# A decoder layer's opening loads put in order of use on one queue, and its constants made during the down projection

## The chip, the cores and the metric

One core of one Trainium2 chip runs the whole kernel. The metric is the device time of one execution in microseconds (us). Matrix products run on TensorE (PE; PEld is its loading of the stationary operand), element-wise work on VectorE (DVE) and ScalarE (ACT). DMAs are issued from the instruction queues of SyncE (SP), ACT and GpSimd (POOL); an issue stands in that engine's order and waits there.

## The reference

One layer of a decoder, 256 tokens of width 2048, all in float32:

```python
h = LN1(ALPHA * x + 0.5 * swiglu(x, ffn1))            # FFN width 5632
mix = mixer(h)      # latent attention beside differential attention, gated and projected
h = LN2(ALPHA * h + mix)
h = LN3(ALPHA * h + 0.5 * swiglu(h, ffn2))

swiglu(x) = (silu(x @ w_gate) * (x @ w_up)) @ w_down
LN(z)     = (z - mean) * rsqrt(var + 1e-5) * g + b
rms(c)    = c * rsqrt(mean(c * c) + 1e-6) * g          # on the latent vectors, on the outputs of the second branch
```

The mixer needs constants that depend on the positions alone: a causal mask, a position bias for each of four heads, the sine and cosine of the rotary angles, and a scalar `lam` from four short vectors.

## The kernel before

**Products.** Each float32 operand is split into a high and a low part (`split`, L148: ACT copies to the PE's rounded type, DVE subtracts), and a product is three matmuls (`triple`, L201). Tokens are two blocks of 128. A weight unit is two k-tiles of 128 by 512 columns, 512 KB; for each unit and block there are six matmuls.

**Units and order.** `project` (L206) walks the units of one 512-column chunk. A unit has four steps: `load` (a DMA on SP into one of four `raw` buffers), `prep` (the split into a pair of a ring of `wring` tiles), the products of block 0, and, as a later step, those of block 1. `lag[0]` says by how many units block 1 may stay behind block 0 (`catch_up`, L163). Each unit ends in a `tick`, and `later(n, f)` puts work n ticks ahead. The program is written in this order; the compiler's scheduler gives each engine its own order from it and issues an instruction sooner if its inputs and a buffer for its output are free. Buffers are taken from pools by tag: `tmp` has six, `sm` 24, `cols` four.

**The opening.** PE first runs 16 matmuls on zeros (`WARM`, L34 and L97). x comes transposed as eight quarters of 256 KB, quarter q of block b by `load_x(q, b)` (L925), issued on ACT's queue: `load_x(0, 0)` before the first unit, the others from `start_hook` at units 1 to 6. The weights come on SP. The first FFN has 22 chunks of gate and up columns; the first two go through `project`, the rest in pairs through `Hybrid.group` (L282), in which part of the work takes seven products in place of eight with sums of weight blocks on DVE (L316).

**Constants.** `setup` (L604) is put 24 ticks ahead at the start (L936), which is in the gate and up stage. It loads the positions, the rotary frequencies, the four short vectors and the gain of the second branch by small DMAs on POOL's queue, and makes the constants on POOL, DVE and ACT.

**Down projection and norms.** `ffn` then sets the ring to four pairs (L571), makes a `LayerNorm` and walks four chunks of 22 units. The LayerNorm loads the residual rows `z` and the gain and shift as rows (`gb`, broadcast to 128 partitions) and, for LN1 and LN2, as columns (`cols`, two DMAs into the `cols` buffers); its `evac` adds each chunk to `z`, and `apply` normalizes, transposes on PE and scales by `cols`. `twice_rstd` (L380) takes one Newton step after a square root and returns twice the reciprocal root, so gains are halved beforehand on ACT (L438, L452, L709) or in `setup` (L658).

**Latent vectors.** In `mixer`, `ckv2_done` (L732) makes the rotary part of the keys, `kr_row`, and puts its transposes on PE (`to_cols`, L672) two ticks ahead.

Of the kernel before, what the change touches and what calls it, by code (L numbers as in the profile page):

```python
# [11 lines left out]
F32 = mybir.dt.float32  # L12
# [6 lines left out]
P = 128  # L19
# [11 lines left out]
G = 2  # L31
SLOTS = 40
LAG = 5
WARM = 16  # L34
# [25 lines left out]
def layer_kernel(ctx: ExitStack, tc: tile.TileContext, a: dict, out: bass.AP):  # L60
# [145 lines left out]
    def project(w, x, k_tiles, width, done, k0=0, hook=None):  # L206
# [15 lines left out]
        def one(j):  # L222
            st = {}

            def load():
                st["raw"] = wpool.tile([P, G * width], F32, tag="raw", name=nm("raw"), bufs=4)
                nc.sync.dma_start(st["raw"], w[j])
# [152 lines left out]
    def twice_rstd(v, eps, n, between=None):  # L380
# [48 lines left out]
    class LayerNorm:  # L429
        def __init__(self, scale, residual, g, bt, each, x=None, cols=None, at=(0, 8)):  # L430
# [41 lines left out]
        def apply(self, b):  # L472
# [5 lines left out]
            if self.cols is None:  # L478
# [3 lines left out]
                r = twice_rstd(mv[:, 1:2], LN_EPS, 1, lambda: center(0))  # L482
# [7 lines left out]
            r = twice_rstd(mv[:, 1:2], LN_EPS, 1)  # L490
# [12 lines left out]
    def ffn(n, x, wgu, wdn, residual, g, bt, each, first=None, nxt=None, cols=None):  # L503
# [52 lines left out]
        project(wgu[0], x, KD, 512, lambda b, bank: gu_done(0, b, bank), hook=first_hook)  # L556
# [47 lines left out]
    def setup():  # L604
# [4 lines left out]
        pos_i = sm(2, "pos_i", I32)  # L609
# [47 lines left out]
        nc.gpsimd.dma_start(subg, a["subln_g"].partition_broadcast(P))  # L657
        V.tensor_scalar(out=subg, in0=subg, scalar1=0.5 * (1.0 - LAMBDA_INIT), scalar2=None, op0=ALU.mult)  # L658
# [45 lines left out]
    def mixer(x):  # L704
# [4 lines left out]
        S.mul(gain, gain, 0.5)  # L709
# [3 lines left out]
        def c_norm(b, i):  # L713
# [6 lines left out]
            r = twice_rstd(ms, RMS_EPS, 1)  # L720
# [11 lines left out]
        def ckv2_done(b, bank):  # L732
# [7 lines left out]
            later(2, lambda: to_cols(kr, krT, b, 2))  # L740
# [70 lines left out]
        def diff_head(h):  # L811
# [24 lines left out]
            def values():  # L836
# [13 lines left out]
                r = twice_rstd(ms, RMS_EPS, 2)  # L850
# [74 lines left out]
    def load_x(q, b):  # L925
        raw = xq.raw(q, b) if q in xq.kept else tmp_tile([P, 512], "xraw")
        nc.scalar.dma_start(raw, a["xT"][q, b])
# [118 lines left out]
```

## Time and profile before

| What | us |
|---|---|
| three runs | 2028.65, 2031.71, 2031.77 |
| median | 2031.71 |
| the profiled execution, its own time | 2028.37 |
| its span, first to last instruction | 2026.6 |
| landing of a 512 KB gate/up weight unit, median of 192 | 4.4 |
| landing of a 256 KB quarter of x, median of 8 | 9.4 |
| idle time of DVE before the splits of weights, waiting for ACT | 409.8 |
| idle time of ACT before the casts of weights, waiting for PE | 540.5 |

The mean TensorE clock granted over the span is 0.997. The last two rows say that over the kernel as a whole ACT and DVE wait for PE to give back ring buffers, not the other way round; where that is not so, the stretches in the prediction show it. A stage is read from its own stretch: the share of busy time over the whole span mixes stages with different limits.

### The profile page before, as it was taken

To read this page: it belongs to the slowest core of one execution; us is meant where nothing else is said; L and a number is where in the kernel's file an instruction comes from. 1 tells how busy PE (TensorE), PEld (TensorE's weight loads), DVE (VectorE), ACT (ScalarE), POOL (GpSimd) and SP (SyncE) were. 2 spreads that over 40 slices of the span, in tenths; PEclk is the share of its full clock that TensorE was granted. 3 is DMA by queue.
4 is the path that set the end of the run, shared out by engine and by line. 5 is a ranking of instruction groups with operands and counts; after the bars stand their busy time and mean duration, and the time that the engine had idled before them with its cause. 6 is when DMAs were issued, how large, how long until landed. Compare 5 with 4: busy or idle time off the path is not lost.

```text
span 2026.6 us, 25079 instructions
## 1 busy us (share of the span) xinstructions
PE 2004.1 (99%) x8984; PEld 1659.3 (82%) x8984; DVE 1527.0 (75%) x1791; ACT 1151.3 (57%) x1443; POOL 218.6 (11%) x409
## 2 busy tenths in 40 slices
PE   8999999999999999999999999999999999999997
PEld 7788888888888887888888888878888888888886
DVE  6999999997554686655665555699999999964555
ACT  5666666676333565555674445476666666653332
POOL 0111001112000012520001100001100100220000
PEclk9999999999999999999999999999999999999999
DMA  8766766668666757874456685666776566686664
GB/s 285 235 223 223 242 227 200 214 218 304 204 195 191 244 183 247 289 246 150 158 167 218 206 282 187 214 232 219 248 248 220 195 216 236 207 309 192 193 196 136
DMA packets 129085, 445.79 MB, mean 220 GB/s; under 512 B 18544, under 2 KB 18624, under 8 KB 128960
## 3 DMA queue, kind: packets, MB, share of 16 engines
q1 hardware_dynamic: 108000, 387.50, 57.3%
q0 software_dynamic: 19808, 54.60, 8.6%
q10 hardware_dynamic: 1152, 2.10, 0.3%
q8 instruction: 70, 1.15, 0.2%
q14 instruction: 55, 0.45, 0.1%
HBM read 419.48 MB, written 24.64 MB: 219 GB/s over the span
## 4 chain that ended last, share of the span: by engine, by line
PE 92%; DMA 3%; DVE 3%; issue 1%; ACT 0%; POOL 0%; DVEq 0%; SPq 0%; ACTq 0%; POOLq 0%
PE mm L202 30%; PE mm L203 30%; PE mm L204 30%; DVE wring L150 1%; DMA xraw<-in_xT_dram 1%; DMA turn<-blocks 1%; DMA sraw<-in_gu_dram 1%; DVE sraw L316 1%; PE tr L370 0%; DMA z<-in_x_dram 0%; ACT wring L149 0%; PE tr L791 0%; PE tr L820 0%; PE tr L789 0%; DVE blocks L405 0%
## 5 line engine op out<-in xcount | busy, mean ns | idle before, releaser
L150 DVE TENSOR_TENSOR wring<-raw,wring 128x1024 fp32r<-128x1024 f32 (+1 forms) x582 | 701.6, 1209 | 409.7 <-ACT wring L149 404.8
L149 ACT CAST wring<-raw 128x1024 fp32r<-128x1024 f32 (+1 forms) x582 | 604.9, 1043 | 547.3 <-PE mm L204 470.1
L202 PE MATMUL mm<-wring,h 128*128 128x512 f32 (+2 forms) x1632 | 634.1, 389 | 0.0
L204 PE MATMUL mm<-wring,h 128*128 128x512 f32 (+2 forms) x1632 | 630.0, 386 | 0.0
L203 PE MATMUL mm<-wring,h 128*128 128x512 f32 (+2 forms) x1632 | 629.4, 386 | 0.7 <-DVE wring L150 0.7
L203 PEld LDWEIGHTS mm<-wring,h 128*128 128x128 f32 x1632 | 306.7, 188 | 62.3 <-DVE wring L150 1.9
L204 PEld LDWEIGHTS mm<-wring,h 128*128 128x128 f32 x1632 | 306.6, 188 | 62.1 <-DVE h L150 1.0
L202 PEld LDWEIGHTS mm<-wring,h 128*128 128x128 f32 x1632 | 306.7, 188 | 61.1 <-ACT h L149 1.0
L149 ACT CAST wring<-sraw 128x1024 fp32r<-128x1024 f32 x280 | 290.1, 1052 | 113.7 <-PE mm L204 70.4
L150 DVE TENSOR_TENSOR wring<-sraw,wring 128x1024 fp32r<-128x1024 f32 x280 | 335.2, 1219 | 7.3 <-ACT wring L149 4.9
L202 PE MATMUL mm<-wring,xs 128*128 128x512 f32 x560 | 218.0, 389 | 1.5 <-ACT snap L293 1.5
L203 PE MATMUL mm<-wring,xs 128*128 128x512 f32 x560 | 218.0, 389 | 0.8 <-DVE wring L150 0.8
L204 PE MATMUL mm<-wring,xs 128*128 128x512 f32 x560 | 217.9, 389 | 0.0
L316 DVE TENSOR_TENSOR sraw<-sraw,sraw 128x1024 f32<-128x1024 f32 x160 | 191.9, 1215 | 0.1
L407 POOL DMA_DIRECT2D hT<-blocks x176 | 95.5, 550 | 744.0 <-DVE blocks L405 739.9
L202 PE MATMUL mm<-wring,x 128*128 128x512 f32 x384 | 150.5, 393 | 4.4 <-ACT x L149 4.4
L203 PE MATMUL mm<-wring,x 128*128 128x512 f32 x384 | 150.1, 392 | 0.3 <-DVE wring L150 0.3
L204 PE MATMUL mm<-wring,x 128*128 128x512 f32 x384 | 150.0, 392 | 0.0
L202 PEld LDWEIGHTS mm<-wring,xs 128*128 128x128 f32 x560 | 105.1, 188 | 23.8 <-ACT snap L293 1.9
L203 PEld LDWEIGHTS mm<-wring,xs 128*128 128x128 f32 x560 | 105.1, 188 | 23.2 <-DVE wring L150 1.3
L204 PEld LDWEIGHTS mm<-wring,xs 128*128 128x128 f32 x560 | 105.1, 188 | 21.6
L407 POOL DMA_DIRECT2D turn<-blocks x104 | 56.6, 551 | 309.9 <-DVE blocks L405 271.1
(238 smaller groups left out, 1619.1 us busy)
## 6 DMA issues: line engine op xcount, KB each, us to landing
raw<-in_gu_dram SPq DMA_DIRECT2D x192, 512.0 KB, 4.4
raw<-in_dn_dram SPq DMA_DIRECT2D x176, 512.0 KB, 4.3
sraw<-in_gu_dram SPq DMA_DIRECT2D x160, 512.0 KB, 5.1
raw<-in_wgm_dram SPq DMA_DIRECT2D x32, 512.0 KB, 3.4
raw<-in_wgd_dram SPq DMA_DIRECT2D x32, 512.0 KB, 3.9
raw<-in_w_out_dram SPq DMA_DIRECT2D x32, 512.0 KB, 3.4
hT<-blocks POOLq DMA_DIRECT2D x176, 64.0 KB, 2.5
hraw<-hT POOLq DMA_DIRECT2D x44, 256.0 KB, 4.1
```

The source lines that it names most:

```text
L149: S.copy(hi, src)
L150: V.tensor_tensor(out=lo, in0=src, in1=hi.bitcast(F32), op=ALU.subtract)
L202: PE.matmul(o, xh, wh, start=first, stop=False, skip_group_check=again)
L203: PE.matmul(o, xh, wl, start=False, stop=False, skip_group_check=again)
L204: PE.matmul(o, xl, wh, start=False, stop=last, skip_group_check=again)
L316: V.tensor_tensor(out=t, in0=t, in1=R[add[1]][s], op=ALU.add)
L407: nc.gpsimd.dma_start(to.rearrange("(g r) (i f) -> i r g f", g=4, i=4)[i], t[32 * i:32 * (i + 1), :].rearrange("r (g f) -> r g f", g=4))
```

## The change

- `WARM` goes from 16 to 12.
- All eight quarters of x are issued on SP's queue, between the weight units in the order of their use: `first_tokens` loads the quarter of block 0 ahead of an even unit, `second_tokens` (through the new argument `between`) that of block 1 just before block 1's products. The first unit is loaded and split in two halves. `lag[0]` is no longer set to 1 at the start, so in the first chunk block 1 follows block 0 unit by unit.
- `setup` is put 26 ticks ahead from the start of the first FFN's down projection. Its `pos_i` and the raw gain of the second branch are now `tmp` tiles.
- `twice_rstd` becomes `rstd`: the square root is taken of four times the value, so that the plain reciprocal root comes out, and the halvings of `cols`, `gb`, `gain` and `subg` go. `cols` is one DMA into a `tmp` tile.
- The transposes of `kr_row` are put four ticks ahead in place of two.

```diff
-WARM = 16
+WARM = 12
...
-    def project(w, x, k_tiles, width, done, k0=0, hook=None):
+    def project(w, x, k_tiles, width, done, k0=0, hook=None, between=None):
...
+            parts = [slice(i * width, (i + 1) * width) for i in range(G)] if between is not None and j == 0 else [slice(0, G * width)]
...
-                nc.sync.dma_start(st["raw"], w[j])
+                for c in parts:
+                    nc.sync.dma_start(st["raw"][:, c], w[j][:, c])
...
-                split(*pair, st["raw"])
+                for c in parts:
+                    split(*(t[:, c] for t in pair), st["raw"][:, c])
...
-            return load, prep, lambda: products(0, j, st["pair"]), lambda: products(1, j, st["pair"])
+            def second():
+                if between is not None:
+                    between(j)
+                products(1, j, st["pair"])
+            return load, prep, lambda: products(0, j, st["pair"]), second
...
-    def twice_rstd(v, eps, n, between=None):
+    def rstd(v, eps, n, between=None):
...
-        S.activation(sd, ve, AF.Sqrt)
+        S.activation(sd, ve, AF.Sqrt, scale=4.0)
...
-        V.tensor_scalar(out=w, in0=v, scalar1=eps, scalar2=-1.0, op0=ALU.add, op1=ALU.mult)
+        V.tensor_scalar(out=w, in0=v, scalar1=eps, scalar2=-4.0, op0=ALU.add, op1=ALU.mult)
...
-                self.cols = [small.tile([P, KD], F32, tag="cols", name=nm("cols"), bufs=4) for _ in range(2)]
-                for t, src in zip(self.cols, cols):
-                    nc.gpsimd.dma_start(t, src)
-                S.mul(self.cols[0], self.cols[0], 0.5)
+                t = tmp_tile([P, 2, KD], "cols")
+                nc.gpsimd.dma_start(t.rearrange("p a k -> p (a k)"), cols)
+                self.cols = [t[:, i, :] for i in range(2)]
...
-                if i == 0:
-                    later(4, lambda: S.mul(t, t, 0.5))
...
-        project(wgu[0], x, KD, 512, lambda b, bank: gu_done(0, b, bank), hook=first_hook)
+        project(wgu[0], x, KD, 512, lambda b, bank: gu_done(0, b, bank), hook=first_hook,
+                between=between)
...
+        if n == 1:
+            later(26, setup)
         for c in range(4):
             project(wdn[c], h, KF, 512, lambda b, bank, c=c: ln.evac(c, b, bank), hook=more if c == 0 else dn_hook(c))
...
-        pos_i = sm(2, "pos_i", I32)
+        pos_i = tmp_tile([P, 2], "pos_i", I32)
...
-        nc.gpsimd.dma_start(subg, a["subln_g"].partition_broadcast(P))
-        V.tensor_scalar(out=subg, in0=subg, scalar1=0.5 * (1.0 - LAMBDA_INIT), scalar2=None, op0=ALU.mult)
+        sg = tmp_tile([P, DV], "sg")
+        nc.gpsimd.dma_start(sg, a["subln_g"].partition_broadcast(P))
+        V.tensor_scalar(out=subg, in0=sg, scalar1=1.0 - LAMBDA_INIT, scalar2=None, op0=ALU.mult)
...
-        S.mul(gain, gain, 0.5)
...
-            later(2, lambda: to_cols(kr, krT, b, 2))
+            later(4, lambda: to_cols(kr, krT, b, 2))
...
-        nc.scalar.dma_start(raw, a["xT"][q, b])
+        nc.sync.dma_start(raw, a["xT"][q, b])
...
-    def start_hook(j):
-        if j in (2, 4, 6):
-            load_x(j // 2, 0)
-        if 1 <= j < 5:
-            load_x(j - 1, 1)
-
-    later(24, setup)
+    def first_tokens(j):
+        if j % 2 == 0:
+            load_x(j // 2, 0)
+
+    def second_tokens(j):
+        if j % 2 == 0:
+            load_x(j // 2, 1)
+
     set_ring(LAG + 5)
-    lag[0] = 1
-    load_x(0, 0)
```

More of the change, by code (lines that the diff above doesn't have):

```diff
@@ L481, in center @@
                                            op0=ALU.subtract, op1=ALU.mult)
-                r = twice_rstd(mv[:, 1:2], LN_EPS, 1, lambda: center(0))
+                r = rstd(mv[:, 1:2], LN_EPS, 1, lambda: center(0))
                 for c in range(4):
@@ L489, in apply @@
                 return
-            r = twice_rstd(mv[:, 1:2], LN_EPS, 1)
+            r = rstd(mv[:, 1:2], LN_EPS, 1)
             for c in range(4):
@@ L501, in apply, with ffn @@
                 later(12 + c, lambda c=c: finish(c))
-    def ffn(n, x, wgu, wdn, residual, g, bt, each, first=None, nxt=None, cols=None):
+    def ffn(n, x, wgu, wdn, residual, g, bt, each, first=None, between=None, nxt=None, cols=None):
         hb = {}
@@ L719, in c_norm @@
             V.tensor_scalar(out=ms, in0=ss, scalar1=1.0 / RANK, scalar2=None, op0=ALU.mult)
-            r = twice_rstd(ms, RMS_EPS, 1)
+            r = rstd(ms, RMS_EPS, 1)
             V.scalar_tensor_tensor(out=c, in0=c, scalar=r, in1=gain[:, i * RANK:(i + 1) * RANK],
@@ L849, in values @@
                 V.tensor_scalar(out=ms, in0=ss, scalar1=1.0 / DV, scalar2=None, op0=ALU.mult)
-                r = twice_rstd(ms, RMS_EPS, 2)
+                r = rstd(ms, RMS_EPS, 2)
                 orow = tmp_tile([P, 512], "orow")
@@ L952, in layer_kernel @@
     h2 = Acts(KD, "h2", (0, 1))
[L953 removed]
+    ln = LayerNorm(1.0, res[0], a["ln2_g"], a["ln2_b"], keep(1), h2, a["ln2_cols"])
     for c in range(4):
```

10 lines of the change are left out of this document (4 added, 6 removed).

## The prediction

> **What bounds the kernel now.** I read the page's engine table and chain first.
>
> ```profile
> PE 2004.1 (99%) x8984; PEld 1659.3 (82%) x8984; DVE 1527.0 (75%) x1791; ACT 1151.3 (57%) x1443; POOL 218.6 (11%) x409
> ...
> PE 92%; DMA 3%; DVE 3%; issue 1%; ACT 0%; POOL 0%; DVEq 0%; SPq 0%; ACTq 0%; POOLq 0%
> ```
>
> TensorE is busy for 2004.1 of 2026.6 us, so everything that this change can win lies in some 22 us: where PE is idle, where its clock is low, and before its first real product. Busy time by stretches shows where (columns: stretch, its length, busy time of PE, PEld, DVE, ACT, POOL, then PE clock, DMA share, GB/s).
>
> ```profile
> core 0: us, PE busy (x) PEld busy (x) DVE busy (x) ACT busy (x) POOL busy (x), PEclk, DMA share, GB/s
> ...
> 7.07:12.76 5.69, 5.37 (x24) 3.86 (x22) 3.13 (x6) 2.62 (x3) 0.00 (x0) 1.00 1.01 313
> 12.76:17.12 4.36, 0.00 (x0) 0.00 (x0) 1.25 (x2) 0.67 (x3) 0.00 (x0) 0.92 1.05 397
> 17.12:23.28 6.16, 6.16 (x15) 4.86 (x16) 5.81 (x8) 6.16 (x11) 0.00 (x0) 0.50 0.40 138
> ...
> 60.00:115.00 55.00, 52.65 (x231) 42.95 (x231) 52.42 (x83) 36.66 (x46) 12.54 (x23) 1.00 0.67 216
> 115.00:470.00 355.00, 355.00 (x1568) 293.87 (x1567) 347.70 (x358) 235.01 (x276) 42.18 (x78) 1.00 0.68 225
> 470.00:510.00 40.00, 39.32 (x173) 31.90 (x172) 25.12 (x29) 23.88 (x27) 10.73 (x20) 1.00 0.90 321
> 510.00:700.00 190.00, 190.00 (x840) 157.39 (x839) 97.82 (x87) 77.83 (x74) 0.00 (x0) 1.00 0.64 205
> ```
>
> The reader is to see: a hole of 4.36 us at 12.76, then 6.16 us in which PE is "busy" at clock 0.50, then 2.35 us lost in 60 to 115, 0.68 lost at the head of the down projection (470 to 510), and nothing in between. What opens the hole is in the timeline (start, duration, instruction, idle time before and what ended it) and, below the dots, in the chain of waits.
>
> ```profile
> 1.06 6.28 PE L98 MATMUL tr<-zero 128*128 128x128 f32 x32 [1.06 <-DVE zero L96]
> 5.02 0.86 ACTq L927 DMA_DIRECT2D xraw<-in_xT_dram  x2
> 11.33 0.33 ACTq L927 DMA_DIRECT2D xraw<-in_xT_dram  x1
> 11.71 1.05 ACT L149 CAST wring<-raw 128x1024 fp32r<-128x1024 f32 x1 [2.91 <-DMA xraw<-in_xT_dram]
> 16.45 2.18 ACT L149 CAST x<-xraw 128x512 fp32r<-128x512 f32 x4 [3.69 <-DMA xraw<-in_xT_dram]
> 17.12 1.22 PE L202 MATMUL mm<-wring,x 128*128 128x512 f32 x2 [4.36 <-ACT x L149]
> ...
> 7.24 9.19 DMA xraw<-in_xT_dram
> ```
>
> A quarter of x issued at 7.24 lands at 16.43. ACT both issues x and casts, in order: its last issue comes as late as 11.33, and the cast behind it stands 2.91 us on x. Weights of later units share the DMA engines meanwhile (SP issues them from 0.74 on, shown below). So PE starves for x, not for weights: what ends its wait at 17.12 is the cast of x.
>
> **The opening, step by step.** After the change one queue carries x00, first weight unit in halves, x01, unit 1, x10, unit 2, x11 and so on. Bytes over time are in the DMA view of the first 40 us (one number per us); durations are in the tile views (min/median/max ns), and the spacing of products at both clocks in PE's timeline.
>
> ```profile
> 0.74 37.95 SPq L227 DMA_DIRECT2D raw<-in_gu_dram  x16
> ...
> GB/s 0 33 279 395 393 375 315 188 187 353 406 363 404 387 387 395 406 418 246 4 0 0 164 352 78 377 184 287 176 188 328 217 315 147 352 373 328 328 16 147
> ...
> L149 ACT CAST x<-xraw x8: 614/616/619, 5.0 to 20.2; 128x512 fp32r<-128x512 f32 x8
> L150 DVE TENSOR_TENSOR x<-xraw,x x8: 684/688/693, 5.7 to 21.7; 128x512 fp32r<-128x512 f32 x8
> ...
> L149 ACT CAST wring<-raw x14: 1029/1046/1057, 5.5 to 39.0; 128x1024 fp32r<-128x1024 f32 x14
> L150 DVE TENSOR_TENSOR wring<-raw,wring x13: 1217/1220/1226, 6.6 to 39.7; 128x1024 fp32r<-128x1024 f32 x13
> DMA to landing us min/median/max: 3.4/4.9/10.8
> ...
> 20.27 0.63 PE L203 MATMUL mm<-wring,x 128*128 128x512 f32 x1
> 20.70 0.63 PE L204 MATMUL mm<-wring,x 128*128 128x512 f32 x1
> ...
> 23.74 0.40 PE L202 MATMUL mm<-wring,x 128*128 128x512 f32 x1
> 23.98 0.39 PE L203 MATMUL mm<-wring,x 128*128 128x512 f32 x1
> ```
>
> Adding up the rate: 312 KB by 3.0 us, 707 by 4, 1100 by 5, 1475 by 6, then about 400 a us. In the new order x00 (262 KB) is moved by 2.9, the first half unit (524) by 3.5, the second (786) by 4.2, x01 by 4.9, unit 1 by 6.2, x10 by 6.9, unit 2 by 8.2. To landing I add 0.9: the shortest landing is 3.4, of which 1.1 passes before bytes flow (0.74 to about 1.9) and 1.3 is a unit's 524 KB. ACT (0.62 per quarter or half unit, 1.05 per unit) and DVE (0.69, 1.22) follow in that order: DVE ends unit 0's second half near 6.4, x01 near 7.1, unit 1 near 9.3, unit 2 near 11.4.
>
> PE: 12 warm matmuls are 24 of the 32 records, 24 x 6.28/32 = 4.7 us, a little more because the early ones are slower; they end near 6.0. Real products start there, not at 7.07: 1.1 won. Six products take 1.4 us, so block 0 and block 1 of unit 0 run to about 8.9, then 0.4 of waiting for unit 1; from 9.3 a unit takes 12 x 0.23 = 2.7 us, while DMA delivers a unit with one quarter in 0.79 MB / 0.4 = 2.0, ACT needs 1.7 and DVE 1.9. Nothing is late after that. Gone are the hole (4.36) and the half clock: spacing 0.43 instead of 0.23 over 6.16 us, 2.9 lost. 1.1 + 4.36 + 2.9 - 0.4 = **8.0 won**. The short wait for the second product before the change (5.37 busy of 5.69) is about what the new halves still leave; I set them equal, and take 0.1 off for a clock that may come up later: 7.9, bounds 4.4 and 8.5.
>
> The costs of this part: SP gets nine more issues, 0.33 to 0.43 us each by the rows above, 3 to 4 us in all, hidden as each issue moves a quarter or half unit that takes 0.65 us of transfer. SP waits in order: x21 stands behind unit 4, which waits for unit 0's buffer (free near 6.4), and all later weights stand behind both; unit 4 is needed near 17, so eight us of cover. The split of unit 0 adds 0.2 us each to ACT and DVE, before PE can start anyway. Block alternation adds no instruction.
>
> **Setup moves to the down projection.** In 60 to 115 DVE is busy 52.42 of 55.00, and setup runs there.
>
> ```profile
> L641 DVE SCALAR_TENSOR_TENSOR ang<-turns,ang 128x128 f32<-128x128 f32 x12 | 3.4, 285 | 0.0
> L623 DVE SCALAR_TENSOR_TENSOR bias<-dist,mask 128x384 f32<-128x384 f32 x4 | 2.0, 553 | 0.0
> ...
> 67.84 9.23 DMA sraw<-in_gu_dram
> ...
> 75.32 1.04 ACT L149 CAST wring<-sraw 128x1024 fp32r<-128x1024 f32 x1 [4.08 <-DMA sraw<-in_gu_dram]
> ...
> invf<-in_inv_freq_dram POOLq DMA_DIRECT2D x1, 16.0 KB, 6.9
> ```
>
> Its two largest groups alone take 5.4 us of a DVE that has 2.6 to spare, and while 16 KB of `invf` needed 6.9 us, a weight block took 9.23 and ACT stood 4.08. I take 2.0 of the 2.35 lost there as won; bounds 0 (the transfer is late for another reason) and 2.35. In 115 to 470, without setup, DVE at 347.70 of 355.00 loses PE nothing.
>
> At the other end nothing hides it for sure. The head of the down projection already runs its DMA at 0.90 and loses 0.68:
>
> ```profile
> 484.58 8.88 DMA z<-in_x_dram
> ...
> 496.79 0.50 PE mm L203
> ...
> 493.48 1.06 ACT L446 ACTIVATE z<-z 128x1024 f32<-128x1024 f32 x1 [1.78 <-DMA z<-in_x_dram]
> ...
> 497.29 1.05 ACT L446 ACTIVATE z<-z 128x1024 f32<-128x1024 f32 x1
> ```
>
> Although `rows` is coded for later ticks, its transfers are issued at 484.58; what has a free buffer is moved ahead. Setup's tiles come from the six `tmp` buffers, free once the last gate/up blocks are stored near 480, so I expect setup at 485 to 510, not near tick 26. There DVE has 40.00 - 25.12 = 14.9 us to spare, but both engines wait in order, and its transfers queue behind z. Price from below: -0.7 (the present wait goes; the halving of `gb` leaves ACT). From above: 6, one more landing such as z's 8.88 less 2.7 of lead (one unit of the ring of four; the others are used up there). I take 2.0 lost: the nearest row is ACT's 4.08 beside the same transfers, of which PE can have lost no more than that stretch's 2.35. If setup does come at tick 26 or later, 510 to 700 shows 97.82 of 190 for DVE and the cost is 0.
>
> **The kr transposes** come two ticks later.
>
> ```profile
> 763.14 1.23 DVE L150 TENSOR_TENSOR wring<-raw,wring 128x1024 fp32r<-128x1024 f32 x1 [0.28 <-ACT wring L149]
> ...
> 765.61 0.56 PE L675 MATMUL tr<-ident,kr_row 128*128 128x128 f32 x2 [1.60 <-DVE kr_row L670]
> ```
>
> PE stands 1.60 us on `kr_row` at the head of its order, although unit 0 of wdq still has six products for block 1 and unit 1's weights are ready at 763.14 + 1.23 = 764.4. Two ticks later the transposes stand some 5.4 us behind, after their input. I take the whole 1.6; bounds 0 (PE then waits for the next weights) and 1.6.
>
> **The rest at nothing.** `rstd` yields half of what `twice_rstd` did, so the halvings of `cols`, `gb` and `gain` go: short ACT work that PE does not wait for in any stretch above but the head of down, where it is counted. `cols` becomes one transfer into a `tmp` buffer held to the end of LayerNorm; the other five suffice in the down projection, whose evacuation uses none. If they did not, setup would only come later, where its cost is 0.
>
> **The sum** against the profiled execution's 2028.37 us (span 2026.6 and 1.8 around it): 7.9 + 2.0 + 1.6 - 2.0 = 9.5 won, 2018.9. The other three runs shown are 2028.65, 2031.71 and 2031.77. A second stretch at half clock of the length seen would cost about those 3 us; the trace cannot say whether that is it. If it hangs on the hole, it goes as well; if not, the median stays 3 above. I add 1: **2020 us**.
>
> **Rivals.**
> (1) *The clock comes up later.* The warm-up is four matmuls shorter and the first products have small gaps. If PE stays at 0.50 for another 6.16 us, 2.9 us go: 2023. For it: the clock in the trace followed PE's pauses. Against: the pauses now are 0.4 us, not 4.36. [...] Chance 0.13.
> (2) *Setup costs more at the head of down.* At the upper bound of 6 the sum is 2024. For it: the DMA share of 0.90 and the 6.9 us for 16 KB of `invf`. Against: z's landing of 8.88 cost PE only 0.68. [...] Chance 0.14.
> (3) *x is not early after all*: the order on SP's queue comes out other than coded (the scheduler moves what has no buffer to wait for), quarters fall behind weights and the hole stays. Then only 1.1 + 2.0 + 1.6 - 2.0 = 2.7 are won: 2026 to 2029 by the runs' spread. Chance 0.06.
> (4) *Slower.* One mechanism: in the head of down DVE, in order, stands first on `row_i`, then on `invf` behind the queue of z and `gb`, and no weight is split meanwhile. Two landings such as z's 8.88 are 17.8, less 2.7 of lead, and the hole of over 4 us halves the clock as it did at 17.12, 2.9 more: 18. Against 11.5 won elsewhere that is 2035 on the profiled time. It decides from a stall of some 11.5 us. Against it: the second to the fourth z, in one queue, were there by 493.48 and 497.29, two microseconds each, so a second transfer does not wait another full 8.88. Chance 0.04.
>
> **How the numbers follow.** Forecast 0.63 with its own range 2016 to 2024; rivals 0.13, 0.14, 0.06, 0.04. The range 2013 to 2027 takes in all gains with setup at -0.7 and the low runs below, and rivals 1 and 2 on the high runs above; about 0.15 is left out. A measurement of this kernel can tell about 0.2%, 4 us, from no change. Forecast and rivals 1 and 2 are faster by more than that on nearly all runs, rival 3 about half: faster 0.89, same 0.07, slower 0.04.
>
> **What would show it.** Right: no PE gap over 1 us before 30 us, the first real product near 6, no clock of 0.50 after it, x landings in order of use; 55 of 55 us busy in the gate/up stretch where setup was; no wait before the kr transposes. Setup's `ang` group in the trace tells where it landed, and PE's idle time there its price. Wrong: a clock row of 0.50 past 10 us, or several PE gaps on `wring` in the first 40 us of the down projection.

## The result and the profile after

| | median us | range | runs |
|---|---|---|---|
| before | 2031.74 | 2028.65 to 2033.45 | 6 |
| after | 2019.2 | 2016.5 to 2025.13 | 6 |

The changed kernel takes **0.9946 of the time before, 95% interval 0.9929 to 0.9962**. The profiled execution took 2019.19 us with a span of 2017.4, against 2028.37 and 2026.6 before: 9.2 us of span went. The medians lie 12.5 us apart, because the profiled execution of the kernel before was faster than all six of its timed runs, while that of the changed kernel stands at their median.

First the engine table of the changed kernel, then its busy time by stretches. The columns are those of the same view before: stretch, length, busy time of PE, PEld, DVE, ACT, POOL, PE clock, DMA share, GB/s.

```profile
PE 1999.8 (99%) x8976; PEld 1656.7 (82%) x8976; DVE 1528.2 (76%) x1792; ACT 1146.0 (57%) x1435; POOL 218.5 (11%) x407
```

```profile
10.00:20.00 10.00, 9.47 (x42) 7.65 (x42) 9.47 (x12) 8.00 (x11) 0.00 (x0) 1.00 1.04 406
...
60.00:115.00 55.00, 55.00 (x244) 45.54 (x244) 51.71 (x51) 36.19 (x42) 6.53 (x12) 1.00 0.76 256
462.00:502.00 40.00, 38.11 (x165) 30.11 (x163) 30.08 (x62) 24.62 (x31) 14.10 (x26) 1.00 0.90 321
502.00:692.00 190.00, 190.00 (x838) 157.31 (x839) 99.44 (x87) 78.81 (x75) 0.00 (x0) 1.00 0.60 206
```

The reader is to see four things. From 10 to 20 us PE is busy for 9.47 us at clock 1.00, where before it stood 4.36 us and then ran at 0.50. Gate/up is full: 55.00 of 55.00. The head of the down projection is worse, 38.11 of 40.00, where the same stretch lost 0.68 before. And the rest of down loses nothing. PE's timeline of the changed kernel (start, duration, instruction, idle time before and what ended it) has the first product, the one pause of the opening, the two pauses at the head of down, and two more that the prediction does not speak of:

```profile
6.20 0.77 PE L202 MATMUL mm<-wring,x 128*128 128x512 f32 x1
...
10.69 0.50 PE L203 MATMUL mm<-wring,x 128*128 128x512 f32 x1 [0.53 <-DVE wring L150]
...
486.23 0.50 PE L203 MATMUL mm<-wring,h 128*128 128x512 f32 x1 [0.81 <-DVE wring L150]
501.92 0.50 PE L203 MATMUL mm<-wring,h 128*128 128x512 f32 x1 [1.04 <-DVE wring L150]
...
829.09 0.50 PE L202 MATMUL mm<-wring,cn 128*128 128x512 f32 x1 [1.21 <-ACT kTr L759]
877.34 0.70 PE L707 MATMUL tr<-ident,p 128*128 128x128 f32 x3 [1.72 <-DVE p L802]
```

There is no wait any more for the transposes of `kr_row`, but PE now stands 1.21 and 1.72 us later on, where it stood 0.54 and 0.36 before. The windows view of the two stretches, of the kernel before and then of the changed one (9 us earlier, for the same work), puts numbers to it; columns are stretch, length, PE busy, clock, DMA share, GB/s.

```profile
760.00:820.00 60.00, 58.40 (x265) 1.00 0.80 260
820.00:900.00 80.00, 79.10 (x355) 1.00 0.82 268
```

```profile
751.00:811.00 60.00, 60.00 (x275) 1.00 0.74 259
811.00:891.00 80.00, 77.07 (x346) 1.00 0.79 268
```

The first row of each pair gives the gain at kr, 60.00 - 58.40 = 1.6; the second gives a loss of 79.10 - 77.07 = 2.0, 70 to 120 us behind it.

The opening by itself comes from a mark further on: the copy of the first bank of the mixer's first projection, the first of these two rows' start times, in the tile views of the kernel before and of the changed one.

```profile
L726 ACT COPY c_row<-mm x2: 586/628/669, 729.4 to 737.8; 128x512 f32<-128x512 f32 x2
```

```profile
L733 ACT COPY c_row<-mm x2: 586/628/671, 720.6 to 729.1; 128x512 f32<-128x512 f32 x2
```

The mark comes 8.8 us earlier. Gate/up gave 55.00 - 52.65 = 2.35 of it, the head of down took (40.00 - 38.11) - 0.68 = 1.2, so the opening gave 8.8 - 2.35 + 1.2 = **7.65**. With kr's 1.6 and the 2.0 behind it that makes 8.4 of the 9.2; the last 0.8 stands in no pause of PE (behind 900 us both kernels show only two, of 0.13 us each) and stays open.

### The profile page after: what moved, and what is told of

It is laid out like the page before. It is cut to its first block, busy times and chain, and to the rows that moved or that the text cites. A ratio compares the mean times of both kernels' runs of the same rounds, so it can differ in the third digit from the quotient of the medians.

```text
span 2017.4 us, 25059 instructions
## 1 busy us (share of the span) xinstructions
PE 1999.8 (99%) x8976; PEld 1656.7 (82%) x8976; DVE 1528.2 (76%) x1792; ACT 1146.0 (57%) x1435; POOL 218.5 (11%) x407
## 4 chain that ended last, share of the span: by engine, by line
PE 94%; DMA 3%; DVE 1%; issue 1%; POOL 1%; ACT 1%; SPq 0%; DVEq 0%; ACTq 0%; POOLq 0%
PE mm L203 31%; PE mm L204 31%; PE mm L202 31%; DMA turned<-turn 1%; DMA turn<-blocks 1%; DMA invf<-in_inv_freq_dram 1%; PE tr L377 0%; POOL turn L414 0%; DMA sg<-in_subln_g_dram 0%; DVE wring L150 0%; DMA raw<-in_gu_dram 0%; ACT wring L149 0%; PE tr L827 0%; DMA raw<-in_wdv_dram 0%; PE tr L707 0%
```

## The experiments

Times are medians; ratios are to the kernel before, run on the same chip. Marks and pauses are each of one profiled execution, which is not always near the median of its runs: small_out's and x_on_act's are the fastest of theirs.

### The opening: order of use, or the small transfers

The change does two things to the first microseconds. It puts x in order on one queue, and, as `pos_i`, `sg` and `cols` become `tmp` tiles and `setup` moves, it takes the six small transfers that POOL issues there (`pos_i`, `subg`, four of `cols`) out of them. The prediction counted the first alone. **open_only** is the kernel before with the first alone; the small transfers stay.

```diff
-WARM = 16
+WARM = 12
-        nc.scalar.dma_start(raw, a["xT"][q, b])
+        nc.sync.dma_start(raw, a["xT"][q, b])
-    ffn(1, xq, ..., keep(0), start_hook, h1, ...)
+    ffn(1, xq, ..., keep(0), first_tokens, second_tokens, h1, ...)
```

> The kernel before with the opening of the change alone (quarters of x between the weights on SP, first unit in halves, alternating blocks, 12 warm matmuls); setup, gains and the kr transposes stay as before. Theory: the opening is worth 7.6 us by itself: no PE hole over 1 us before 30 us, first product near 6.2, no clock of 0.50 after 7 us; the 2.35 us lost in gate/up, 0.7 at the head of the down projection and 1.6 before the kr transposes all stay. About 2021 us by the profile. Rival: much of the opening's gain comes from the small transfers of the constants leaving POOL's queue at the start (pos_i, subg, cols were issued there from 2.06 us on). Then x and the first weights still land late here, PE waits 2 us or more before 15 us, and about 2024 us result.

2025.29 us (2022.79 to 2027.2, 10 runs), ratio 0.9975, interval 0.9965 to 0.9984: less than half of what the change gives. Its timelines of POOL (the first and the last of the six issues), of ACT and of PE, its mark, then the DMA view of its first 40 us (one number a microsecond):

```profile
2.06 0.68 POOL L618 DMA_DIRECT2D pos_i<-in_pos_col_dram  x1
...
4.85 0.53 POOL L444 DMA_DIRECT2D cols<-in_ln_bc_dram  x1
...
9.89 0.62 ACT L149 CAST x<-xraw 128x512 fp32r<-128x512 f32 x1 [3.23 <-DMA xraw<-in_xT_dram]
...
10.56 0.50 PE L202 MATMUL mm<-wring,x 128*128 128x512 f32 x1 [2.38 <-ACT x L149]
```

```profile
L734 ACT COPY c_row<-mm x2: 586/630/674, 725.2 to 733.6; 128x512 f32<-128x512 f32 x2
```

```profile
DMA  0389797989999999999999977038887897782789
GB/s 0 41 281 270 193 330 125 132 296 413 368 385 388 387 408 389 389 340 391 404 389 340 315 242 291 16 61 319 213 299 205 250 291 254 274 348 107 98 299 410
```

And the same view of the changed kernel:

```profile
DMA  0197899999999999999993049594987696999999
GB/s 0 23 328 250 238 332 383 389 410 399 406 422 404 406 393 412 399 408 399 414 389 127 12 94 373 209 315 172 307 213 225 250 385 176 315 389 361 389 397 393
```

In the seventh and eighth microsecond the DMA engines of open_only are busy 7 and 9 tenths and move 125 and 132 GB/s; in the changed kernel they are busy 9 and 9 tenths and move 383 and 389. The quarter x01 comes late by that, in spite of its place in the order, and PE stands 2.38 us; the clock then falls to 0.50 for 3.41 us. The rival held.

**small_out** is the other half: the changed kernel with the opening of before put back.

```diff
-WARM = 12
+WARM = 16
-        nc.sync.dma_start(raw, a["xT"][q, b])
+        nc.scalar.dma_start(raw, a["xT"][q, b])
-    def first_tokens(j):
...
+    def start_hook(j):
+        if j in (2, 4, 6):
+            load_x(j // 2, 0)
+        if 1 <= j < 5:
+            load_x(j - 1, 1)
+
     set_ring(LAG + 5)
+    lag[0] = 1
+    load_x(0, 0)
```

> The changed kernel with the opening of before put back: quarters of x on ACT's queue, issued by the hook of before, one lag, no alternation of token blocks, 16 warm-up products; setup stays in down and keeps its temporary tiles, so that the small transfers of constants are not in the opening. Theory (the small transfers slow every transfer while they run, so a good part of the opening's gain comes without any new order of x): the holes of the opening shrink by 3 to 5 us against before, and with the 2.35 us of gate/up and less the 1.2 us at the head of down the time is 2021 to 2023 us. Rival (the order of use makes the gain, the small transfers only move holes): the opening loses as much as before to within 1 us, and the time is 2025 to 2027 us.

2023.98 us (2020.35 to 2027.82, 6 runs), ratio 0.9964 [0.995, 0.9978]. The mark of the mixer's first bank and the pause of the opening:

```profile
15.13 0.73 PE L202 MATMUL mm<-wring,x 128*128 128x512 f32 x2 [2.18 <-ACT x L149]
```

```profile
L733 ACT COPY c_row<-mm x2: 586/630/674, 724.5 to 732.9; 128x512 f32<-128x512 f32 x2
```

The mark is 4.9 us earlier than before. Less 2.35 for gate/up and plus 1.3 for a head of down that lost 0.80 + 1.18, the opening gave 3.85. For open_only the same sum (mark at 725.2, 4.2 earlier, less 0.25 and 0.26 for pauses that were a little shorter in gate/up and at the head of down) gives 3.7. **Each half alone gives a half, 3.7 and 3.85; both give 7.65.** The hole of 4.36 us needed both causes, and either one leaves a pause of 2.2 to 2.4 us that still costs a stretch of half clock. By medians the shares come out alike, 4.7 and 5.1 of 10.3; from the last two 9.2 - 7.65 = 1.55 is taken off for what lies outside the opening, and the changed kernel's median is that of its second set of runs, below. Of the two expectations the theory's holds for the pauses; its time, 2021 to 2023, was missed by 1 us.

**x_on_act** leaves everything in place but the queue.

```diff
-        nc.sync.dma_start(raw, a["xT"][q, b])
+        nc.scalar.dma_start(raw, a["xT"][q, b])
```

> The changed kernel with only the queue of the quarters of x changed: they are issued by ACT, in the same place of the program, and so no longer stand between the weights on SP's queue. Theory of the prediction (one queue in order of use decides): quarters and weights compete, the first product or a unit of weights comes later, at least one pause over 1 us appears in the first 15 us, and the time is 2020.5 to 2023 us. Rival (what counts is the place in the program and the absence of the small transfers; the queue is worth nothing): no pause over 1 us in the first 15 us, and the time is within 1 us of 2019.2.

2023.02 us (2021.46 to 2023.47, 4 runs), ratio 0.9959 [0.9944, 0.9974]. The chain of waits and PE's timeline:

```profile
8.47 6.20 DMA xraw<-in_xT_dram
...
15.37 0.50 PE L202 MATMUL mm<-wring,x 128*128 128x512 f32 x1 [2.62 <-ACT x L149]
```

A pause of 2.62 us and a stretch at 0.50: about the time of small_out. The order of the program, without the one queue that keeps it, is worth nothing here. The first row above, of the chain of waits, says why: the quarter that PE waits for is issued only at 8.47, on ACT's queue, behind a cast that itself waited for weights until 7.81. It then takes 6.20 us to land, no longer than the median of 6.7 in the changed kernel. So here it is late because ACT issues it late, more than because weights share the DMA engines with it; the prediction names both. Its step that one queue keeps the order of use held.

**warm16** puts the four warm-up products back.

```diff
-WARM = 12
+WARM = 16
```

> The changed kernel with 16 warm-up products instead of 12. Theory (the warm-up ends before the first product's inputs are there, so its length is worth nothing): the time is within 1 us of the changed kernel on the same chip, and the clock comes up at the same distance from the first warm-up product. Rival (the longer warm-up stands in front of the first real products on PE): the first real product comes 0.8 us or more later than at 6.2 us, and the time is 0.8 us or more longer.

2018.66 us (2017.05 to 2020.5, 4 runs), ratio 0.9943 [0.9928, 0.9958], the same as the changed kernel on the same chip (below). The first real product comes at 7.31, 1.1 us later than 6.20 as the rival had it, but the time does not grow:

```profile
7.31 0.47 PE L202 MATMUL mm<-wring,x 128*128 128x512 f32 x1
```

Its mark stands at 719.5, no later than 720.6. The early start is paid back by the 0.53 us pause at 10.16, which warm16 has not, and by the first products at a clock that in the changed kernel rises only at 6.89. Neither expectation is whole: the product moves, the time does not, as far as intervals of 3 us in width can tell.

### Setup: where it lands, and what costs there

**setup_early** is the changed kernel with setup put at the start again, its tiles still the `tmp` ones.

```diff
-        if n == 1:
-            later(26, setup)
...
+    later(24, setup)
     set_ring(LAG + 5)
```

> The changed kernel with setup put back 24 ticks after the start, in the gate and up stage; all else as changed. Theory: setup itself costs PE in gate/up, since DVE is full there: 1 to 2.4 us of PE idle time come back between 50 and 110 us, and the head of the down projection loses 0.7 or less in place of 1.9. Span within 1.5 us of the changed kernel's 2017.4. Rival: the loss in gate/up came from the late opening, not from setup: no PE gap over 0.5 us there, and the span is 1 us or more below 2017.4.

2020.46 us in a single run, span 2018.7. Gate/up loses again and the head of down loses nothing:

```profile
52.00:107.00 55.00, 52.95 (x227) 43.34 (x226) 51.32 (x85) 35.51 (x45) 12.76 (x23) 0.97 0.67 211
...
462.00:502.00 40.00, 40.00 (x177) 32.95 (x176) 26.10 (x30) 23.22 (x28) 11.38 (x21) 1.00 0.90 324
```

So both terms are setup's, and the theory held. How it costs PE there is in the timelines of DVE and of PE:

```profile
66.56 0.30 DVE L623 CAST posrow<-row_i 128x256 f32<-128x256 int32 x1 [3.68 <-DMA row_i<-in_pos_row_dram]
...
69.70 0.50 PE L202 MATMUL mm<-wring,xs 128*128 128x512 f32 x1 [2.05 <-ACT snap L300]
```

DVE stands 3.68 us on `row_i`, ACT stands 3.54 on what DVE makes of it, and the copy `snap` that PE waits for is behind that on ACT. It is one pause, of 2.05 us, and a stretch of half clock from 70.51 on (the 0.97) comes on top. In the kernel before the pauses of this stage look otherwise: 1.52 us behind a weight block that lands late, and 0.83. (The opening of setup_early stays clean, though setup is coded at the start: the `tmp` tiles alone keep its transfers out of the first microseconds.)

In the changed kernel setup starts at 472 us, not 26 ticks on: `pos_i`, `row_i` and `invf` are issued between the transfers of z and `gb`. What it does there is in the timelines of DVE and ACT of the changed kernel:

```profile
484.75 0.29 DVE L625 CAST posrow<-row_i 128x256 f32<-128x256 int32 x1 [3.64 <-DMA row_i<-in_pos_row_dram]
...
495.32 1.05 ACT L149 CAST wring<-raw 128x1024 fp32r<-128x1024 f32 x1 [5.17 <-DMA raw<-in_dn_dram]
496.39 1.28 ACT L660 ACT_TABLE_LOAD   x1
...
497.90 1.28 ACT L464 ACT_TABLE_LOAD   x1
```

DVE stands 3.64 us on `row_i`, with splits of weights behind it, and PE pays 0.81 of that at 485.43. The second pause, 1.04 us at 500.89, has more than one root. ACT stands 5.17 us on weights, but in setup_split below, without setup's transfers, it stands almost as long there and PE loses nothing:

```profile
492.93 1.05 ACT L149 CAST wring<-raw 128x1024 fp32r<-128x1024 f32 x1 [4.02 <-DMA raw<-in_dn_dram]
```

What the changed kernel has besides is setup's work in front of the next splits. ACT loads the table of a function twice, 1.28 us each (for the exponential of `lam`, then for a square root of LayerNorm), before its next cast at 499.31, and DVE works on `ang` until just before the split at 500.65 that PE waits for. No run separates these shares.

**setup_late** holds setup's five inputs with a one-element write from a finished bank (the 128x512 sums of one block and chunk), so that the transfers cannot be issued before down's first chunk ends, near 521 us.

```diff
+        def dn_done(c, b, bank):
+            if n == 1 and c == 0 and b == 1:
+                hold(bank)
+                later(1, setup)
+            ln.evac(c, b, bank)
...
+    def hold(bank):
+        for name, shape, dt in (("pos_i", [P, 2], I32), ...):
+            t = held[name] = tmp_tile(shape, name, dt)
+            V.tensor_copy(t[:, 0, 0:1] if len(shape) == 3 else t[:, 0:1], bank[:, 0:1])
```

> The changed kernel, but setup's five input tiles are first written by DVE from the first finished down chunk, so that its transfers and its work cannot start before about 525 us. Theory: PE's loss at the head of the down projection falls from 1.9 to 0.7 or less, since setup's work and transfers took weights' time there, and in the second chunk the full ring hides setup: no PE gap over 0.3 us between 510 and 690. Span 1.2 to 1.9 us below 2017.4 plus what the opening varies. Rival: DVE and ACT wait in order for setup's transfers there too, and PE loses 1 us or more in the second chunk; or the loss at the head comes from z and gb alone and stays at 1.9.

2018.49 us (2017.45 to 2020.35, 4 runs), ratio 0.9936 [0.9916, 0.9956]. The head of down is free of pauses, but:

```profile
525.66 0.17 DVE L630 CAST pos<-pos_i 128x2 f32<-128x2 int32 x1 [1.35 <-DMA pos_i<-in_pos_col_dram]
...
532.53 1.22 DVE L150 TENSOR_TENSOR wring<-raw,wring 128x1024 fp32r<-128x1024 f32 x1
...
533.80 0.50 PE L203 MATMUL mm<-wring,h 128*128 128x512 f32 x1 [1.35 <-DVE wring L150]
```

Even in a stretch where DVE is idle half of the time (99.44 of 190.00 us busy in the changed kernel) the price is 1.35 us. The rival's pause came, but its reason, DVE and ACT waiting in order for setup's transfers, is only a part. These waits (1.35 us on `pos_i`, 0.74 on `row_i`) hold the split at 526.98. The split that PE waits for, at 532.53, has had its cast since 528.85; in between DVE works on setup's constants, with a wait of 0.52 on a transfer among them.

**setup_split** takes the waits away: it issues the transfers at 521 and holds the computation until the second chunk is finished. Its edit is shown against setup_late's.

```diff
             if n == 1 and c == 0 and b == 1:
                 hold(bank)
-                later(1, setup)
+            if n == 1 and c == 1 and b == 1:
+                setup(bank)
...
+        V.tensor_copy(pos[:, 0:1], bank[:, 0:1])
         V.tensor_copy(pos, pos_i)
```

> The changed kernel with the constants split in two: the five transfers are issued when down's first chunk is finished (near 521 us), and the computation is held until its second chunk is finished some 45 us later, so that DVE and ACT find the data landed. Theory (it is the wait of DVE and ACT, in order behind a transfer that has not landed, that costs PE, not the 3 to 5 us of computation): no PE pause over 0.5 us from 460 to 690 us, the 1.9 us of the two pauses at the head of down are won, and the span is 2015 to 2016 us. Rival (the computation itself delays the emptying of banks): a pause of 0.7 to 1.5 us near 570 us, span 2016.5 to 2017.5 us.

2017.98 us (2015.85 to 2019.77, 4 runs), ratio 0.9935 [0.9919, 0.9952]; the profiled span is 2015.4. No wait of DVE or ACT for a transfer of setup is left, and yet:

```profile
462.00:502.00 40.00, 40.00 (x178) 33.11 (x178) 23.87 (x26) 22.24 (x25) 11.39 (x21) 1.00 0.91 332
```

```profile
588.61 0.50 PE L203 MATMUL mm<-wring,h 128*128 128x512 f32 x1 [1.06 <-DVE wring L150]
```

One pause of 1.06 us at 587.55 stays: from 580 us on DVE works almost without a break on setup and on the emptying of banks, where it has 1.5 us free per unit (12 products at 0.23 us, less a split of 1.22), and the next split starts at 587.33, 5.9 us after the cast that it follows has ended. So the computation itself costs PE, without any wait for a transfer. The rival's pause came (0.7 to 1.5 near 570); of the 1.9 us, 0.8 were won. The theory's span came too, but the pause near 876, 0.76 here where the changed kernel has 1.72, gave 1.0 of it.

**spread** cuts that computation into five parts, each behind a finished bank of chunks two to four.

```diff
+        return {(1, 0): distances, (1, 1): biases, (2, 0): lambda bank: stage(0, bank),
+                (2, 1): lambda bank: stage(1, bank), (3, 0): rest}
...
+            if n == 1 and (c, b) in pieces:
+                pieces[c, b](bank)
```

> The changed kernel with the transfers of the constants near 521 us and their computation in five parts, each held until a finished bank of down's second, third and fourth chunk, so that each part is 1 to 2.5 us of DVE. Theory (what is left of the price of setup is a run of DVE work between two splits that is longer than the 1.5 us that DVE has free per unit): no PE pause over 0.4 us from 460 to 690 us, 1.9 us less than the changed kernel, a span of 2015 to 2016 us. Rival (a run of 2 us is still too long, or the finished banks come late by it): one to three pauses of 0.5 to 1 us at 577 to 670 us, span 2016 to 2017.5 us.

> The changed kernel once more, beside the versions below on one chip: 2018 to 2020 us as before, with the pauses near 485, 501, 828 and 876 us. Every theory expects the same; it is the base for the next two.

The changed kernel again: 2019.28 us (2016.77 to 2020.46, 5 runs), ratio 0.9943 [0.9931, 0.9956]. spread: 2019.41 us (2017.54 to 2021.1, 5 runs), ratio 0.9945 [0.9933, 0.9958], no better. The pause of setup_split is gone, but one piece, the scaling of `subg`, has no hold of its own and went ahead:

```profile
530.95 0.29 DVE L690 TENSOR_SCALAR subg<-subg 128x256 f32<-128x256 f32 x1 [5.33 <-DMA subg<-in_subln_g_dram]
...
532.43 0.50 PE L203 MATMUL mm<-wring,h 128*128 128x512 f32 x1 [0.77 <-DVE wring L150]
```

DVE stood 5.33 us on one transfer and PE 0.77. Three pauses of 0.2 to 0.5 us at 714 to 717, at the transposes of LayerNorm, and one of 0.76 at 797 are new too; that the last part of setup delays the three behind it is likely and was not tried. Neither expectation held, and whether five parts that are all held would cost nothing stays open.

### kr, and the two pauses behind it

**kr_two** is the changed kernel with the transposes of kr two ticks ahead again.

```diff
-            later(4, lambda: to_cols(kr, krT, b, 2))
+            later(2, lambda: to_cols(kr, krT, b, 2))
```

> The changed kernel with the kr transposes two ticks ahead again. Theory: PE stands about 1.6 us before the kr transposes near 754 us, and the two later waits of the changed kernel (1.21 us before products with cn near 828, 1.72 before the first transposes of p near 876) shrink towards the 0.54 and 0.36 of the kernel before, since they wait for a chain of transfers that does not come sooner: net under 1 us. Rival: the later waits are the schedule's own and stay at 1.2 and 1.7; then the span is 1.6 us above the changed kernel's.

2019.8 us in a single run, span 2018.0, only 0.6 over the changed kernel's. PE's timeline and its windows:

```profile
757.11 0.71 PE L683 MATMUL tr<-ident,kr_row 128*128 128x128 f32 x2 [2.63 <-DVE kr_row L678]
...
831.64 0.50 PE L202 MATMUL mm<-wring,cn 128*128 128x512 f32 x1 [0.36 <-ACT kTr L759]
```

```profile
811.00:891.00 80.00, 79.64 (x359) 65.60 (x358) 47.87 (x64) 46.38 (x68) 33.12 (x61) 1.00 0.84 273
```

The wait for kr is back (2.63, and a stretch of half clock after it), and the later waits go from 2.93 (80.00 - 77.07) to 0.36. In these two profiles what is won at kr is lost behind it: PE arrives earlier at work whose inputs come no sooner. The other profiles bear this out with one exception. PE's wait for kr and its pauses from 820 to 890 us add up to 2.43 to 2.99 in the three kernels with two ticks (before, open_only, kr_two), and to 1.95 to 3.25 in nine with four (spread_wide, with other steps, is left aside); small_out, with four, has only 0.47, and no run says why.

**heads_later** moves all steps of the first branch's heads two units back.

```diff
-                later(12 + 3 * h + 2 * i, f)
+                later(14 + 3 * h + 2 * i, f)
```

> The changed kernel with every step of the eight heads of the first mixer branch two units later. Theory (the pauses of 1.21 us at 828 and 1.72 us at 876 are products and transposes placed ahead of chains that don't come sooner): the pause at 876 falls under 0.4 us, that at 828, which is of a product of a projection on turned columns, goes or moves with kT, and the span is 2015.5 to 2016.5 us. Rival (the chain of turns by transfers sets the time, and work that comes later only moves the pause on): pauses of the same sum come within 30 us behind, the span is 2017 to 2018 us.

2018.77 us (2017.22 to 2018.97, 4 runs), ratio 0.9938 [0.992, 0.9955]. PE pauses 1.68 us at 880.58 in place of 1.72 at 875.62. The rival held, the pause moved. DVE's and ACT's timeline of the changed kernel show why:

```profile
872.13 1.05 ACT L149 CAST wring<-raw 128x1024 fp32r<-128x1024 f32 x1 [2.64 <-DMA raw<-in_wdv_dram]
...
873.21 1.23 DVE L150 TENSOR_TENSOR wring<-raw,wring 128x1024 fp32r<-128x1024 f32 x1 [2.30 <-ACT wring L149]
874.35 0.55 DVE L688 SCALAR_TENSOR_TENSOR st<-tr,mask 128x384 f32<-128x384 f32 x1
...
877.00 0.55 DVE L802 TENSOR_SCALAR p<-p,rs 128x128 f32<-128x128 f32 x2
```

The softmax (`st` at 874.35, `p` done at 877.55: 3.2 us) stands on DVE behind a split that waits for a cast that waits for late weights of `wdv`. Moving scores and transposes together leaves their distance at two units.

**spread_wide** is spread with three units between the steps of a head.

```diff
-                later(12 + 3 * h + 2 * i, f)
+                later(12 + 3 * h + 3 * i, f)
```

> The version before with the three steps of a head of the first mixer branch three units apart instead of two, so that softmax has one unit more before its transposes. Theory (the pause at 876 us is a transpose that waits for its own softmax, some 2.9 us of chain behind the scores, and not for a transfer): no pause over 0.4 us near 876 to 900 us, 1 to 1.7 us less than the version before. Rival (the pause only moves, as when all steps came two units later): a pause of 1 us or more between 870 and 905 us, and a time within 0.5 us of the version before.

**2016.55 us** (2015.41 to 2018.23, 5 runs), ratio 0.9931 [0.9919, 0.9944]. The windows of spread and of spread_wide:

```profile
860.00:900.00 40.00, 38.17 (x179) 31.49 (x178) 24.12 (x41) 23.83 (x41) 11.07 (x20) 1.00 0.74 236
```

```profile
860.00:900.00 40.00, 40.00 (x193) 33.77 (x192) 26.81 (x43) 24.77 (x42) 10.98 (x20) 1.00 0.74 236
```

The pause is gone and 1.83 us with it; the medians differ by 2.9. The theory's number held, with more won than it said. One profile does not settle it, as kr_two, small_out and warm16 show no pause near 876 either, with steps two units apart. Beside the changed kernel on the same chip, five runs each, it is 2.7 us faster by medians; the intervals of the two ratios overlap (0.9919 to 0.9944, 0.9931 to 0.9956), so this is likely, not settled. It is the fastest version of these runs. The same spacing without spread's move of setup was not tried.

## Why the prediction was right, step by step

- **The opening** was put at 7.9 won (bounds 4.4 and 8.5); it gave 7.65. The clock, the first product near 6 (6.20) and no gap over 1 us before 30 came as said. The order of landings did up to x01; x10 then came behind units 2 and 3, which had a free buffer to go to, and cost nothing that PE's timeline shows. What failed is the reason: the step has PE starve because ACT issues x late and "Weights of later units share the DMA engines meanwhile", and leaves out the small transfers that POOL issues in the same microseconds. By open_only and small_out they are half of it. In the changed kernel the two causes went together, so the sum came out; for the order of x alone the prediction would have been wrong by some 4 us. The rate row of before showed it already, 188 and 187 GB/s in the eighth and ninth microsecond with 395 four microseconds earlier; the prediction added that row up and did not ask why it dips.
- **"1.1 won"** by four warm-up products fewer, a part of the 7.9, was worth nothing that warm16 shows. The products that follow stood or ran slowly for about as long.
- **Gate/up**: 2.0 predicted, 2.35 measured, all of the loss, and setup_early brings it back. The bound was right, the choice below it too careful. The reason given first, a DVE with 2.6 us to spare, was misread: the 52.42 already hold setup's 5.4. In setup_early it is a wait in order, of DVE on `row_i`, that costs PE, and in the kernel before a late weight block is behind the longer pause.
- **The head of down**: 2.0 lost predicted, 1.2 measured. Setup did come ahead of its tick, at 472 to 502; the 485 to 510 expected are 475 to 500 in the changed kernel's time, which runs 10 us ahead there. ACT and DVE did stand on transfers. The size was taken from ACT's 4.08 in gate/up; here DVE stood 3.64 and ACT 5.17, and a ring of four covered most of both. Setup's own price is 1.9, less the 0.68 that went. The prediction took setup's work as covered by the 14.9 us that DVE has to spare; in setup_split, further on, the work alone costs 1.06. One sign of being wrong, several pauses on `wring` in the first 40 us of down, showed itself with 0.81 and 1.04: the sign did not leave room for the loss that the sum already had.
- **kr**: the wait of 1.6 went wholly, as the step has it. That it would stay won was the error: 2.0 came back as longer pauses at 828 and 876. The step asked what stands in front of the transposes and not what PE then reaches earlier. In the end it came to nothing: -0.4 by the windows, +0.6 by kr_two's span.
- **The sum**: 9.5 predicted, 9.2 measured, with errors of -0.25, +0.35, +0.8 and -2.0 in the four terms and 0.8 in no term. That it is so near is in part luck. The 1 us added for the spread of runs made 2020 against a median of 2019.2; the 3 us by which the median of before stood above its profile did go, and the last section shows what they go with.
- **Rivals.** The clock did not come up late: it rose at 6.89, 0.7 us after the first product, and fell only when PE's work was over, behind 2006.7. It rises at another time in every profile, from 5.50 to 7.20 (6.21 in the kernel before). The 0.1 that the sum takes off for a later clock was the author's estimate and no run shows it as a term; what shows is that the changed kernel's first product, ahead of that rise, took 0.77 us, where most of those behind it take 0.39 or 0.40. Setup did not cost 6 at the head of down and x was early. The waits of the slower rival came, on `row_i` 3.64 us and on `invf` 0.68, but nothing near the stall of 11.5 us from which it decides.

## What to carry to other kernels

Look at what else uses the DMA engines in the microseconds that a reordering is to mend: a busy DMA row beside a low rate (7 and 9 tenths at 125 and 132 GB/s in open_only) was here the sign of small transfers, and moving those was worth as much as the order (3.85 and 3.7 us). DVE, with its splits behind the consumer of a late input, paid for it in the two places named here, and PE with it: 3.64 us on `row_i` at the head of down cost PE 0.81, 5.33 on `subg` in the second chunk 0.77. So issue the transfer early and hold the consumer. The work cost too where it was longer than DVE's free time per unit (5.9 us against 1.5 in setup_split, 1.06 of PE); that shorter pieces cost nothing is not shown. And when a wait is taken away, follow PE to the next place where its input comes by a chain of fixed length: here the 1.6 us won at kr came back, by the windows, as 2.0 at 828 and 876.

## What the runs showed that was not expected

The clock fell to 0.50 after pauses of PE as short as 1.8 us. Seven profiles other than that of before have a stretch at 0.50 ahead of the kernel's end, behind pauses of 1.80 us (after_again), 1.90 (setup_late), 2.05 (setup_early), 2.18 (small_out), 2.38 (open_only), 2.62 (x_on_act) and 2.63 (kr_two). None follows the pause of 1.72 in the changed kernel, nor one of 1.83 in spread. In x_on_act the stretch lasts from 17.04 to 20.45, in after_again from 877.48 to 880.90. In the kernel before the clock stands at 1.00 for 10.24 us from 6.21 on, at 0.50 for 6.83 and at 1.00 for 1996.80; in the changed kernel it stands at 1.00 for 2003.62 us from 6.89 on. These are 3, 2, 585 and 587 times 3.413 us. Cut in steps of that length, the stretch ahead of a fall can be read in the windows view. The changed kernel's pause of 1.72 us first, then the same kernel again with 1.80 us; the last number but two is the clock.

```profile
873.87:877.28 3.41, 1.75 (x8) 1.00 1.01 395
877.28:880.69 3.41, 3.35 (x16) 1.00 0.61 213
```

```profile
874.06:877.47 3.41, 1.61 (x9) 0.98 (x8) 2.07 (x8) 2.43 (x6) 0.61 (x1) 1.00 0.97 386
877.48:880.90 3.42, 3.42 (x10) 2.65 (x9) 1.88 (x2) 0.80 (x2) 0.00 (x0) 0.50 0.77 254
```

PE is busy 1.75 us of 3.41 ahead of no fall and 1.61 ahead of one; in x_on_act it is 1.66 ahead of one. In the kernel before the step in its hole, 13.04 to 16.45, has no PE at all and a fall behind it; every other such step at full clock ahead of 2000 us, in its profile and in that of the changed kernel, has 1.81 us of PE or more and no fall. The seven falls follow steps with 1.24 to 1.77 us of PE. So with about half of a step busy both occur, a fall at 1.77 and none at 1.75, and the runs show no sharp bound. PE's ends are modelled, which may be the reason. On the way back, in the kernel before a step at 0.50 with 2.74 us of PE was followed by another at 0.50, in kr_two one with 2.80 us by 1.00.

A stretch of 3.41 us at half clock costs some 1.7 us more, an estimate from its length and the 0.50. The same pause cost this in one profile of the changed kernel, with 1.80 us, and not in the other, with 1.72. The author's reading, that it hangs on where the steps lie, as the first rise comes at another time in every profile, was not tried.

Most of the spread between the runs of the kernel before goes with this clock. Each timed run lists the mean clock that it was granted, and 31 runs of that kernel, made beside the experiments, average 2033.5 us at 0.995, 2030.8 at 0.996, 2029.3 at 0.997 and 2027.3 at 0.998. That is 2.1 us for each 0.001, and 0.001 of the span is 2.0. Which pauses make it is not known, as these runs have no profile.
